# A state-space block that steps four tokens at a time, in a two-block transformer kernel

## The chip, the cores and the metric

The kernel runs on one core of one Trainium2 chip. The metric is the device time of the whole kernel in microseconds. A core has TensorE (PE in the profile), VectorE (DVE), ScalarE (ACT), GpSimd (POOL) and SyncE (SP); the last one here issues nearly all transfers between HBM and SBUF. Each engine runs its own instructions in the order in which the program lists them and waits on semaphores for the others.

## The reference

The program computes two blocks of a network for 256 tokens of width 1024. The first block is FFN, mixer, FFN and a gated embedding; the mixer projects the tokens and feeds a sparse attention (nsa, 8 heads) and a state-space path (s5), whose outputs are joined and projected by `w_out`. The second block has two layers with a context of 256 tokens; its context projections need nothing of the first block. The change concerns the state space:

```python
def s5_mixer(u, a_re, a_im, log_dt, b_re, b_im, c_re, c_im, d_skip, w_glu, b_glu):
    uf = u.reshape(B, L, S5_GROUPS, S5_GROUP)             # 32 groups of 16 channels
    a_bar = jnp.exp(lam * dt)                             # 64 complex states per group
    b_coef = (a_bar - 1.0) / lam
    bu = lax.complex(bu_re, bu_im) * b_coef
    _, state = lax.associative_scan(combine, (a_seq, bu), axis=1)   # x[t] = a x[t-1] + bu[t]
    y = real(state) @ c_re - imag(state) @ c_im + d_skip * uf
    y = jax.nn.gelu(y.reshape(B, L, S5_WIDTH))
    return y * jax.nn.sigmoid(y @ w_glu + b_glu)
```

## The kernel before

Activations lie transposed, channels on partitions and the 256 tokens along the free axis. A large product is made of three fp32r matmuls per weight tile (`mm3`, L360 to L363): high half times high half, high times low, low times high. `split` (L334) loads a weight tile `raw` through SP, ScalarE rounds it to `hi` (L349), and the low half `lo` = raw - hi is made by VectorE or, in every fourth tile of the mixer (`EV_MX` = 4, `self.every`), by GpSimd (L355).

`mixer_in` (L587) normalises h (`sumsq`, `rstd`; the sum over partitions is the matmul `bs`, its input is GpSimd's `acc`), projects u (`ev_u` writes `uT`, L619), then q, k and v (`mmb`, `mma` with `Ah`/`Al`), and then calls `s5` (L744), `nsa` (L844), `ctx_proj` of the second block, and after them `glu` (L796) and the output projection `mmo` (L652 to L655).

`s5` handles 16 pairs of groups, four in each of four steps j. Two matmuls `pbu` give the real and imaginary input of 128 states (two groups of 64) for 256 tokens. VectorE multiplies by the cosine and sine of the state's phase (`s5co`, `s5si`: a rotating frame in which the recurrence is real), GpSimd adds the pairs (L776, L777), two scans over 256 tokens run on VectorE (L780, L781), four products rotate back, GpSimd adds (L787, L788), and two matmuls `psy` multiply with the output matrix. A gelu writes the result over `uT`.

`nsa` first makes compressed keys and values (`compress`: 16 matmuls `cps` each, on weights `cw`), their softmax (`psc`, `pst`), and then for each i of four head pairs and each t of two token halves: scores `psS` (PE), mask and maximum (VectorE, L930), exponentials (ScalarE, L935), division and gate (VectorE, L937 to L941), transposes `psT` (PE), a copy `pT` (ScalarE), the product with the values `psO` (PE), and the halves `Ah`, `Al` of the result (L959, L960).

The order of the work on each engine is set at build time by a scheduler that goes through the program's instructions by priority (program order) and its own durations, within what buffers allow. A pool hands out its buffers in program order, and a tile waits until the tile that had the buffer is released. The PSUM pool `sm` has two buffers and serves `bs`, `psr`, `cps`, `psc`, `pst`, `psT` and `psO` alike; `mm` has two for `mmb`, `mma`, `mmo`; `s5p` holds `pbu` and `psy`. The matmuls of `ctx_proj` (`mmb` and `mma` with `Bh`/`Bl`, 384 and 96 of them) depend on nothing of the mixer and stand in PE's order wherever there is room. At the mixer's end `wmod` (L1020 and after) of the second block streams in, into memory that the attention used; `after` and `gate` (L1063 to L1068) tie such loads to an earlier instruction.

Of the kernel before, what the change touches and what calls it, by code (L numbers as in the profile page):

```python
# [137 lines left out]
def _layout(i):  # L138
# [48 lines left out]
    b = np.zeros((4, 4, 2, 16, 2, 2, 64), np.float32)  # L187
    c = np.zeros((2, 64, 16, 2, 2, 16), np.float32)
    for r, nm in enumerate(("re", "im")):
        bb = i[f"s5_b_{nm}"][0].reshape(4, 4, 2, 64, 16)  # L190
        cc = i[f"s5_c_{nm}"][0].reshape(16, 2, 16, 64)
        for gg in range(2):
            b[:, :, gg, :, r, gg, :] = bb[:, :, gg].transpose(0, 1, 3, 2)
            c[gg, :, :, r, gg, :] = cc[:, gg].transpose(2, 0, 1)
    a["s5b"] = b.transpose(1, 2, 3, 0, 4, 5, 6).reshape(128, 4, 2, 128)
    a["s5c"] = c.reshape(128, 16, 2, 32)
# [43 lines left out]
class Kern:  # L240
# [346 lines left out]
    def mixer_in(self, h, p):  # L587
# [54 lines left out]
        with (  # L642
            tc.tile_pool(name="s5", bufs=2) as sp,
            tc.tile_pool(name="nsa", bufs=2) as np_,
            tc.tile_pool(name="s5p", bufs=1, space=PSUM) as self.s5p,
        ):
# [1090 lines left out]
```

## Time and profile before

| | us |
|---|---|
| median of 3 runs (lowest to highest) | 1577.16 (1574.52 to 1580.79) |
| the profiled execution, its time | 1584.19 |
| the profiled execution, its span | 1582.0 |
| TensorE busy | 1513.8 |
| VectorE busy | 1183.3 |
| ScalarE busy | 873.7 |
| GpSimd busy | 356.9 |
| mean granted TensorE clock | 0.984 |

All rows that follow come from one profiled execution, and times in them count from the start of its span. Busy time of PE is modelled at its end and overlaps weight loads (PEld, the loading of the stationary operand); where PE works without a gap, weight loads are as dense as matmuls, so PEld shows how full PE is. The landmarks of the stretch that the change rewrites are: u is projected from about 206, the last matmul of the projections starts at 253.34, the first matmul of the GLU at 427.23, and the attention's last instruction at 443.36.

### The profile page before, as it was taken

What the parts mean: (1) busy time and instruction counts of PE and PEld (TensorE: products, weight loads), DVE (VectorE), ACT (ScalarE), POOL (GpSimd) and SP (SyncE); (2) the same over time, 40 slices, a digit from 0 to 9 for tenths busy, and PEclk for the clock granted to TensorE, in tenths of its full rate; (3) what the DMA queues carried; (4) which work ended last, traced back from release to release, by engine and by line L of the source; (5) the groups of instructions that cost most, each with busy time, mean ns of one, the idle gap of its engine ahead of it and who ended that gap; (6) DMA issues with size and microseconds to landing.
All of it is one profiled execution on the core that took longest, in us unless ns stands there. A gap on an engine that the chain in (4) does not pass through costs nothing.

```text
span 1582.0 us, 28967 instructions
## 1 busy us (share of the span) xinstructions
PE 1513.8 (96%) x11058; PEld 1401.6 (89%) x11058; DVE 1183.3 (75%) x2103; ACT 873.7 (55%) x1563; POOL 356.9 (23%) x378
## 2 busy tenths in 40 slices
PE   7999999999989999998999899999999989999997
PEld 7999997676677999998999888989999889989997
DVE  7998778898778865666997767677766575777665
ACT  7644556445464554564454567675555555755553
POOL 3320145554331201031021232310030522200100
PEclk9999999999999999999999999999999999999999
DMA  7988565321178636668888664445466444544564
GB/s 262 321 305 293 171 207 166 109 80 62 48 241 297 212 127 181 193 193 296 274 285 255 199 196 149 159 149 164 140 210 195 155 146 161 166 155 127 160 183 144
DMA packets 100523, 298.19 MB, mean 188 GB/s; under 512 B 14944, under 2 KB 23520, under 8 KB 99744
## 3 DMA queue, kind: packets, MB, share of 16 engines
q1 hardware_dynamic: 99056, 290.66, 57.3%
q0 software_dynamic: 1328, 5.68, 1.1%
q8 instruction: 87, 1.43, 0.3%
q14 instruction: 52, 0.43, 0.1%
HBM read 292.10 MB, written 4.20 MB: 187 GB/s over the span
## 4 chain that ended last, share of the span: by engine, by line
PE 70%; DVE 13%; issue 4%; ACT 4%; DMA 4%; POOL 3%; SPq 0%; DVEq 0%; ACTq 0%; POOLq 0%
PE mmm L363 6%; PE mmm L361 6%; PE mmm L362 6%; PE mmb L363 4%; PE mmb L362 4%; PE mmb L361 4%; DVE lo L355 4%; PE mmf L362 4%; PE mmf L363 4%; PE mmf L361 4%; PE mma L362 3%; PE mma L361 3%; PE mma L363 3%; PE mm L362 1%; PE mm L361 1%
## 5 line engine op out<-in xcount | busy, mean ns | idle before, releaser
L355 DVE TENSOR_TENSOR lo<-raw,hi 128x1024 fp32r<-128x1024 f32 (+3 forms) x483 | 549.9, 1141 | 226.8 <-ACT hi L349 225.2
L349 ACT CAST hi<-raw 128x1024 fp32r<-128x1024 f32 (+4 forms) x495 | 474.7, 963 | 403.6 <-PE mmm L362 80.9
L362 PE MATMUL mmb<-Bl,hi 128*128 128x256 f32 x576 | 167.8, 292 | 3.2 <-DVE Bl L409 3.2
L363 PE MATMUL mmb<-Bh,lo 128*128 128x256 f32 x576 | 167.9, 292 | 2.1 <-POOL lo L355 2.0
L361 PE MATMUL mmb<-Bh,hi 128*128 128x256 f32 x576 | 167.2, 292 | 2.7 <-DVE sdk L1302 2.4
L363 PE MATMUL mmm<-Bh,lo 128*128 128x256 f32 x576 | 163.6, 284 | 0.4 <-DVE lo L355 0.4
L361 PE MATMUL mmm<-Bh,hi 128*128 128x256 f32 x576 | 163.0, 283 | 0.3 <-DVE sgmg L1324 0.3
L362 PE MATMUL mmm<-Bl,hi 128*128 128x256 f32 x576 | 162.5, 282 | 0.0
L361 PEld LDWEIGHTS mmb<-Bh,hi 128*128 128x128 f32 x576 | 111.1, 194 | 8.1 <-issue 6.1
L363 PEld LDWEIGHTS mmb<-Bh,lo 128*128 128x128 f32 x576 | 111.6, 194 | 7.3 <-issue 3.9
L362 PEld LDWEIGHTS mmb<-Bl,hi 128*128 128x128 f32 x576 | 111.5, 194 | 7.3 <-DVE Bl L409 3.6
L361 PE MATMUL mmf<-Ah,hi 128*128 128x256 f32 x352 | 100.2, 285 | 10.0 <-ACT Ah L415 7.9
L363 PEld LDWEIGHTS mmm<-Bh,lo 128*128 128x128 f32 x576 | 108.5, 188 | 0.7 <-DVE lo L355 0.6
L361 PEld LDWEIGHTS mmm<-Bh,hi 128*128 128x128 f32 x576 | 108.6, 188 | 0.5 <-DVE sgmg L1324 0.5
L362 PEld LDWEIGHTS mmm<-Bl,hi 128*128 128x128 f32 x576 | 108.5, 188 | 0.0
L361 PE MATMUL mmf<-Bh,hi 128*128 128x256 f32 x352 | 100.8, 286 | 4.5 <-ACT hi L349 4.5
L1039 DVE CUSTOM_DVE_ANT_0 mw<-mw,cb 128x1024 f32<-128x1024 f32 x72 | 90.5, 1258 | 18.2 <-DMA mw<-wmod 13.1
L363 PE MATMUL mmf<-Bh,lo 128*128 128x256 f32 x352 | 100.7, 287 | 1.6 <-DVE lo L355 1.5
L361 PE MATMUL mm<-gh,hi 128*128 128x256 f32 x352 | 99.8, 284 | 1.8 <-DVE fo L545 1.8
L362 PE MATMUL mm<-gl,hi 128*128 128x256 f32 x352 | 99.6, 283 | 1.8 <-DVE gl L526 1.8
L362 PE MATMUL mmf<-Al,hi 128*128 128x256 f32 x352 | 100.4, 285 | 0.3 <-DVE Al L416 0.3
L363 PE MATMUL mmf<-Ah,lo 128*128 128x256 f32 x352 | 100.2, 285 | 0.3 <-DVE lo L355 0.3
(564 smaller groups left out, 4343.4 us busy)
## 6 DMA issues: line engine op xcount, KB each, us to landing
raw<-w SPq DMA_DIRECT2D x120, 512.0 KB, 5.0
raw<-wB SPq DMA_DIRECT2D x76, 512.0 KB, 3.8
mw<-wmod SPq DMA_DIRECT2D x72, 512.0 KB, 5.1
raw<-wml SPq DMA_DIRECT2D x72, 512.0 KB, 3.5
raw<-wbo SPq DMA_DIRECT2D x72, 256.0 KB, 2.7
raw<-wo SPq DMA_DIRECT2D x24, 512.0 KB, 4.3
raw<-w SPq DMA_DIRECT2D x16, 384.0 KB, 4.0
raw<-w_inB SPq DMA_DIRECT2D x12, 512.0 KB, 4.1
```

The source lines that it names most:

```text
L349: nc.scalar.copy(hi[:, :n], raw[:, :n])
L355: eng.tensor_tensor(lo[:, :n - cut], raw[:, :n - cut], hi[:, :n - cut].bitcast(F32), op=ALU.subtract)
L361: nc.tensor.matmul(ps, lh, rh, start=start, stop=False)
L362: nc.tensor.matmul(ps, lh, rl, start=False, stop=False)
L363: nc.tensor.matmul(ps, ll, rh, start=False, stop=stop)
L1039: nc.vector.tensor_tensor_reduce(o, w, cb[:, j - j0, :], 1.0, 0.0, ALU.mult, ALU.add, mod[:, m, j:j + 1])
```

## The change

Four tokens become one step. The tokens of a channel are regrouped so that the four of a step (s) lie on different partitions and the 64 steps (k) along the free axis: `ev_u` writes `uT` in the order (s, k), and the new `s5_load` sends it to HBM (`s5d`) and back into `u4`, 32 channels by four tokens on the 128 partitions, with one write and four reads for each half of the channels, on SP. From powers of a up to the fourth, `s5_setup` builds `z`; for each j, `s5` builds from `x` and `z` the input tables `bx` and the output tables `cx` (VectorE: `s5m`, then sums and differences on 64 partitions), transposes `bx` (`s5pt`, copied by ScalarE to `s5br4`), and multiplies `bx` with `cx` for what tokens of one step give to each other (`s5pk`, copied into `tw`). Both `s5pt` and `s5pk` take their PSUM from `sm`. Then 8 matmuls `pbu` of 64 columns, the rotation, two scans over 4 x 64 columns (with `rt` zero at each first column), the rotation back, and 12 matmuls `psy`. All pair sums are on VectorE. The result goes back to `uT` through HBM, one write and four reads for each two j, on GpSimd's queue, still in the order (s, k); `glu` puts the tokens in order while it reads. `EV_MX` is 0, so GpSimd makes no low half in the mixer. The pool of `s5` is opened ahead of the projections, and `compress` takes its weight buffers from the tag `pT` instead of `cw`.

```diff
@@ flags @@
-EV_CB, EV_B2, EV_F2, EV_MX = 0, 0, 0, 4
+EV_CB, EV_B2, EV_F2, EV_MX = 0, 0, 0, 0
@@ mixer_in @@
+        s5 = contextlib.ExitStack()
+        sp = s5.enter_context(tc.tile_pool(name="s5", bufs=1))
+        self.s5p = s5.enter_context(tc.tile_pool(name="s5p", bufs=1, space=PSUM))
...
         def ev_u(i, ps):
-            nc.vector.tensor_tensor(uT[:, 2 * i:2 * i + 2, :], ps, rb2, op=ALU.mult)
+            nc.vector.tensor_tensor(uT[:, 2 * i:2 * i + 2, :].rearrange("p a (s k) -> p a k s", s=4),
+                                    ps.rearrange("p a (k s) -> p a k s", s=4),
+                                    rstd.rearrange("p (k s) -> p k s", s=4)[:, None].to_broadcast([128, 2, 64, 4]),
+                                    op=ALU.mult)
+            self.s5_load(sp, uT, i)
@@ s5_load, new @@
+        js = slice(2 * jj, 2 * jj + 2)
+        d = self.s5d[jj]
+        self.nc.sync.dma_start(d, uT[:, js, :])
+        for k in range(4):
+            self.nc.sync.dma_start(self.u4[32 * k:32 * k + 32, js],
+                                   d[:, :, 64 * k:64 * k + 64].rearrange("(q c) j k -> c j q k", q=4))
@@ s5, tables of one j @@
+            for ri in range(2):
+                m = [sp.tile([128, 5, 8, 16], F32, tag=f"s5m{n}", name="s5m", bufs=1) for n in range(2)]
+                for n in range(2):
+                    tt(m[n], x[:, n, pr].rearrange("p a b c -> p (a b) c")[:, None].to_broadcast([128, 5, 8, 16]),
+                       z[:, n ^ ri, :, pr, :].rearrange("p s a b -> p s (a b)")[:, :, :, None].to_broadcast([128, 5, 8, 16]),
+                       ALU.mult)
+                for g in range(2):
...
+                    tt(bx[ri][gs, :, :, gc], v[0][gs, 0, :, 0:4, :], v[1][gs, 0, :, 0:4, :], op)
+                    tt(cx[ri][gs, :, :, gc], v[0][gs, 1], v[1][gs, 1], op)
+            for ri in range(2):
+                pt = self.sm.tile([128, 512], F32, tag="sm", name="s5pt")
+                for q in range(4):
+                    nc.tensor.transpose(pt[:, 128 * q:128 * q + 128], bx[ri][:, q].rearrange("p s c -> p (s c)"), ident)
+                nc.scalar.copy(br[:, ri], pt.rearrange("p (a b) -> p a b", a=4))
+            pt = self.sm.tile([128, 512], F32, tag="sm", name="s5pk").rearrange("p (a b) -> p a b", a=4)
...
+            for k in range(4):
+                ks = slice(32 * k, 32 * k + 32)
+                nc.scalar.copy(tw[ks, :, 32 * k:], pt[0:32, :, 0:128 - 32 * k])
@@ s5, pair sums (G is GpSimd, V and tt VectorE) @@
-                G.tensor_tensor(t1, t1, t2, op=ALU.add)
-                G.tensor_tensor(t3, t3, t4, op=ALU.subtract)
...
+            tt(t1, t1, t2, ALU.add)
+            tt(t3, t3, t4, ALU.subtract)
@@ s5, the way back @@
+            if j % 2:
+                js = slice(j - 1, j + 1)
+                d = self.s5d[2 + j // 2]
+                nc.gpsimd.dma_start(d, u4[:, js].rearrange("p j q k -> p j (q k)"))
+                for q in range(4):
+                    nc.gpsimd.dma_start(uT[32 * q:32 * q + 32, js, :].rearrange("c j (s k) -> c j s k", s=4),
+                                        d[:, :, 64 * q:64 * q + 64].rearrange("(s c) j k -> c j s k", s=4))
@@ compress @@
-            raw = p.tile([128, 4, T], F32, tag="cw", name="cw", bufs=2)
+            raw = p.tile([128, 4, T], F32, tag="pT", name="cw")
```

How instructions move, at three places. On PE, in the middle of the stretch of the state space, the first attention half-blocks of the kernel before stand between the context matmuls (`mmb` with `Bh`) and the state space (`pbu`, `psy`):

```order
L363 MATMUL mmb_4761<-Bh_2356,lo_4794 128x256
L361 MATMUL mmb_4761<-Bh_2356,hi_4793 128x256
L953 MATMUL psO_4059<-pT_4082,vtok_2749 128x2x128 x2
L955 MATMUL psO_4059<-pcT_4057,vcm_4017 128x2x128
L948 MATMUL psT_4115<-cst0_97,s__4092 128x128
L770 MATMUL pbu_3688<-uT_2746,braw_2474 128x256 x2
L948 MATMUL psT_4115<-cst0_97,s__4092 128x128 x2
L789 MATMUL psy_3603<-s5u1_3632,cr_2477 32x256
L948 MATMUL psT_4115<-cst0_97,s__4092 128x128
L928 MATMUL psS_4140<-kk_2748,qT_2747 128x128
L928 MATMUL psS_4145<-kk_2748,qT_2747 128x128
L790 MATMUL psy_3603<-s5u3_3634,ci_2478 32x256
```

In the changed kernel, PE at the last tables of the state space and the first `cps` of the compressed keys:

```order
L804 MATMUL s5pk_3682<-s5cx1_3335,s5bx1_3333 32x128
L357 MATMUL mmb_4760<-Bh_2360,hi_4792 128x256
L358 MATMUL mmb_4760<-Bl_2361,hi_4792 128x256
L359 MATMUL mmb_4760<-Bh_2360,lo_4793 128x256
L357 MATMUL mmb_4760<-Bh_2360,hi_4792 128x256
L358 MATMUL mmb_4760<-Bl_2361,hi_4792 128x256
L359 MATMUL mmb_4760<-Bh_2360,lo_4793 128x256
L357 MATMUL mmb_4760<-Bh_2360,hi_4792 128x256
L358 MATMUL mmb_4760<-Bl_2361,hi_4792 128x256
L359 MATMUL mmb_4760<-Bh_2360,lo_4793 128x256
L822 MATMUL pbu_3706<-s5u4_2899,s5br4_3669 128x64 x7
L905 MATMUL cps_3776<-cw_3777,blk_3767 30x256 x4
```

and PE after the GLU's last matmul, where the attention now stands:

```order
L953 MATMUL psc_3878<-kcm_3816,qT_2763 128x15 x8
L953 MATMUL psc_3887<-kcm_3816,qT_2763 128x15 x8
L977 MATMUL pst_3911<-cst0_97,pcm_3898 128x128 x4
L1015 MATMUL psT_3942<-cst0_97,s__3919 128x128 x4
L995 MATMUL psS_3999<-kk_2764,qT_2763 128x128
L995 MATMUL psS_4004<-kk_2764,qT_2763 128x128
L1020 MATMUL psO_3918<-pT_3941,vtok_2765 128x2x128 x2
L1022 MATMUL psO_3918<-pcT_3916,vcm_3876 128x2x128
L1015 MATMUL psT_3974<-cst0_97,s__3951 128x128 x4
L995 MATMUL psS_4031<-kk_2764,qT_2763 128x256
L995 MATMUL psS_4036<-kk_2764,qT_2763 128x256
L1015 MATMUL psT_3980<-cst0_97,s__3951 128x128 x4
```

What moved: in the kernel before `cps` of k begins with the end of the projections and the attention is spread over the rows of the context matmuls; now `cps` of k follows the last `s5pk`, and the eight half-blocks, but for some first scores, follow the GLU with 18 `mmo` matmuls between them.

On VectorE, around the evacuation of u (`uT`), before:

```order
L355 TENSOR_TENSOR lo_2972<-raw_2970,hi_2971 128x1024
L466 RECIPROCAL rstd_2794<-sd_2795 128x256
L355 TENSOR_TENSOR lo_3012<-raw_3010,hi_3011 128x1024
L612 TENSOR_TENSOR cosr_2811<-cst3_2744,rstd_2794 128x256
L613 TENSOR_TENSOR sinr_2812<-cst3_2744,rstd_2794 128x256
L619 TENSOR_TENSOR uT_2746<-mmb_2815,rstd_2794 128x512
L619 TENSOR_TENSOR uT_2746<-mmb_2877,rstd_2794 128x512
L355 TENSOR_TENSOR lo_3082<-raw_3080,hi_3081 128x1024
```

and now, with the tables of j = 0 and the first product of j = 1 (`s5m`) ahead of it:

```order
L770 TENSOR_TENSOR s5bx1_3333<-s5m_3350,s5m_3351 64x16x16
L438 TENSOR_SCALAR rc_2819<-psr_2816 128x2
L770 TENSOR_TENSOR s5cx1_3335<-s5m_3350,s5m_3351 64x20x16
L818 SCALAR_TENSOR_TENSOR s5ph_3386<-cst0_97,s5r_2423 128x256
L351 TENSOR_TENSOR lo_2938<-raw_2936,hi_2937 128x1024
L816 TENSOR_SCALAR s5co_3384<-s5co_3384 128x256
L611 TENSOR_TENSOR cosr_2833<-cst3_2760,rstd_2810 128x256
L612 TENSOR_TENSOR sinr_2834<-cst3_2760,rstd_2810 128x256
L770 TENSOR_TENSOR s5m_3444<-s5x_2476,s5z_2499 128x640
L770 TENSOR_TENSOR s5m_3445<-s5x_2476,s5z_2499 128x640
L602 TENSOR_SCALAR rch_2822<-rc_2819 128x2
L617 TENSOR_TENSOR uT_2762<-mmb_2837,rstd_2810 128x2x64x4
```

What moved: the low half and the evacuation stand behind products and sums of the tables (`s5m`, `s5bx`, `s5cx`), which the kernel before did not have; most of the tables of j = 0 stand in the 20 rows above these.

On GpSimd, before, at the end of the state space (`L312` loads constants of the second block):

```order
L788 TENSOR_TENSOR s5u3_3852<-s5u3_3852,s5u4_3853 128x256
L776 TENSOR_TENSOR s5t1_3862<-s5t1_3862,s5t2_3863 128x256
L777 TENSOR_TENSOR s5t3_3864<-s5t3_3864,s5t4_3865 128x256
L787 TENSOR_TENSOR s5u1_3879<-s5u1_3879,s5u2_3880 128x256
L788 TENSOR_TENSOR s5u3_3881<-s5u3_3881,s5u4_3882 128x256
L355 TENSOR_TENSOR lo_5141<-raw_5139,hi_5140 128x1024
L312 DMA cst1_5444<-cst1 128x516
L1068 COPY cb_6510<-go_320 128x1
```

and now, the whole way back between two memsets and the same load:

```order
L930 MEMSET hidv_3819 128x512
L958 MEMSET pcm_3898 128x512
L854 DMA s5d2_112<-s5u4_2899 128x512
L856 DMA uT_2762<-s5d2_112 32x8x64 x4
L854 DMA s5d3_113<-s5u4_2899 128x512
L856 DMA uT_2762<-s5d3_113 32x8x64 x4
L308 DMA cst1_5303<-cst1 128x516
L1135 COPY cb_6369<-go_324 128x1
```

What moved: the sums are gone from GpSimd, and ten transfers stand ahead of the load of constants.

## Rows read from the trace of the kernel before

**Rows 1.** The page: busy time and instructions by engine; the chain that ended last.

```profile
PE 1513.8 (96%) x11058; PEld 1401.6 (89%) x11058; DVE 1183.3 (75%) x2103; ACT 873.7 (55%) x1563; POOL 356.9 (23%) x378
...
PE 70%; DVE 13%; issue 4%; ACT 4%; DMA 4%; POOL 3%; SPq 0%; DVEq 0%; ACTq 0%; POOLq 0%
```

**Rows 2.** Busy us, instructions by stretch, then granted clock, DMA share, GB/s.

```profile
60.00:180.00 120.00, 118.19 (x988) 118.02 (x987) 103.19 (x185) 56.63 (x82) 16.20 (x18) 0.99 0.81 279
225.00:253.50 28.50, 28.50 (x213) 25.36 (x211) 19.96 (x34) 17.65 (x27) 9.29 (x7) 1.00 0.51 157
253.50:427.20 173.70, 168.53 (x857) 115.58 (x856) 153.45 (x352) 88.81 (x176) 88.06 (x78) 0.95 0.29 91
...
475.00:520.00 45.00, 41.47 (x203) 34.03 (x203) 39.22 (x69) 21.52 (x41) 8.32 (x5) 1.00 0.85 291
```

**Rows 3.** Single PE instructions (start, us); PE's waits; one stretch at half clock.

```profile
253.57 2.34 PE L838 MATMUL cps<-cw,blk 128*30 128x256 f32 x10
...
426.88 0.60 PE L948 MATMUL psT<-cst,s__4291 128*128 128x128 f32 x4
...
PE pbu L770 <- DVE s5t L746: 1.7, 1, 1.7
...
355.00:360.00 5.00, 5.00 (x21) 3.63 (x21) 5.00 (x16) 0.59 (x1) 2.64 (x4) 0.50 0.32 105
```

**Rows 4.** VectorE's groups, 253 to 428: count, busy us, mean ns, idle before.

```profile
L355 DVE TENSOR_TENSOR lo<-raw,hi 128x1024 fp32r<-128x1024 f32 x18 | 24.3, 1352 | 1.8 <-ACT hi L349 1.8
L780 DVE TENSOR_TENSOR_SCAN s5zr<-s5r,s5t 128x256 f32<-128x256 f32 x16 | 14.1, 879 | 0.0
...
L746 DVE TENSOR_TENSOR s5u<-s5zi,s5co 128x256 f32<-128x256 f32 x16 | 11.9, 746 | 0.0
...
L746 DVE TENSOR_TENSOR s5u<-s5zr,s5si 128x256 f32<-128x256 f32 x16 | 6.6, 410 | 0.0
```

**Rows 5.** GpSimd's groups, 200 to 470.

```profile
L355 POOL TENSOR_TENSOR lo<-raw,hi 128x1024 fp32r<-128x1024 f32 x11 | 28.5, 2593 | 34.7 <-ACT hi L349 34.7
...
L787 POOL TENSOR_TENSOR s5u<-s5u,s5u 128x256 f32<-128x256 f32 x16 | 16.5, 1029 | 43.6 <-DVE s5u L746 43.6
```

**Rows 6.** Single instructions of GpSimd and VectorE, 256 to 266.

```profile
256.12 2.38 POOL L355 TENSOR_TENSOR lo<-raw,hi 128x1024 fp32r<-128x1024 f32 x1 [3.63 <-ACT hi L349]
...
256.61 2.18 DVE L765 TENSOR_SCALAR s5co<-s5co 128x512 f32<-128x512 f32 x1 [0.31 <-ACT s5co L764]
...
265.43 0.41 DVE L765 TENSOR_SCALAR s5co<-s5co 128x512 f32<-128x512 f32 x1
```

**Rows 7.** GpSimd's DMA issues (ns min/median/max); its transfers, us to landing.

```profile
L312 POOL DMA_DIRECT2D cst<-cst x2: 600/604/609, 208.3 to 442.7; - x2
...
pT<-pT POOLq DMA_DIRECT2D x1, 256.0 KB, 4.8
```

**Rows 8.** Groups of the attention on VectorE, then on ScalarE.

```profile
L960 DVE TENSOR_TENSOR Al<-psO,Ah 64x256 fp32r<-64x256 f32 x5 | 2.1, 417 | 0.4 <-ACT Ah L959 0.4
...
L930 DVE CUSTOM_DVE_ANT_0 s__4246<-psS,cst 128x256 f32<-128x256 f32 x4 | 1.6, 398 | 0.0
...
L941 DVE TENSOR_TENSOR s__4246<-s__4246,l 128x1024 f32<-128x1024 f32 x1 | 1.2, 1211 | 0.0
...
L949 ACT COPY pT<-psT 128x512 f32<-128x512 f32 x12 | 7.0, 582 | 16.3 <-PE psT L948 16.2
...
L935 ACT ACTIVATE s__4246<-s__4246,mx 128x256 f32<-128x256 f32 x4 | 2.0, 496 | 1.7 <-DVE mx L932 1.7
...
L935 ACT ACTIVATION_READ_ACCUMULATOR s__4246<-s__4246,mx 128x1 f32 x4 | 0.7, 187 | 0.0
```

**Rows 9.** The u evacuation on VectorE: start, us of both.

```profile
222.69 1.28 DVE L619 TENSOR_TENSOR uT<-mmb,rstd 128x512 f32<-128x512 f32 x2
```

**Rows 10.** The attention's last instruction, and the first load of wmod.

```profile
443.36 0.43 DVE L960 TENSOR_TENSOR Al<-psO,Ah 64x256 fp32r<-64x256 f32 x1
...
443.91 0.43 SPq L1035 DMA_DIRECT2D mw<-wmod  x1
```

More of the change, by code (lines that the diff above doesn't have):

```diff
@@ L158, in _layout @@
     put("bglu", _cols(i["s5_b_glu"][0]))
-    put("s5d", _cols(i["s5_d"][0].reshape(-1)))
+    put("s5d", np.tile(i["s5_d"][0].reshape(16, 32).T, (4, 1)))
     put("are", _cols(i["s5_a_re"][0].reshape(-1)))
@@ L186, in _layout @@
     a["wcv2"] = i["cmp_wv2"][0].reshape(2, 128, 64).transpose(1, 0, 2)
-    b = np.zeros((4, 4, 2, 16, 2, 2, 64), np.float32)
-    c = np.zeros((2, 64, 16, 2, 2, 16), np.float32)
+    x = np.zeros((2, 64, 2, 16, 2, 16), np.float32)
     for r, nm in enumerate(("re", "im")):
[L190 to L196, printed above, removed]
+        x[:, :, r, :, 0] = i[f"s5_b_{nm}"][0].reshape(16, 2, 64, 16).transpose(1, 2, 0, 3)
+        x[:, :, r, :, 1] = i[f"s5_c_{nm}"][0].reshape(16, 2, 16, 64).transpose(1, 3, 0, 2)
+    a["s5x"] = x.reshape(128, 2, 16, 2, 16)
     a["wglu"] = _wb(i["s5_w_glu"][0])
@@ L281, in run @@
             self.spill = [dram.tile([128, 8, T], F32, name=f"spill{n}") for n in range(2)]
+            self.s5d = [dram.tile([128, 2, T], F32, name=f"s5d{n}") for n in range(4)]
             self.grow = dram.tile([8, 128], F32, name="grow")
@@ L641, in mixer_in @@
         opair = self.new_pair(8, "A")
[L642 to L646, printed above, removed]
+        with s5, tc.tile_pool(name="nsa", bufs=2) as np_:
             self.s5(sp, uT)
@@ new lines, in s5_setup, with cmul @@
+        nc.scalar.copy(P[:, 1, 1], s1)
+        tmp = [tp.tile([128, 5, 16], F32, tag=f"s5tm{n}", name="s5tm", bufs=1) for n in range(2)]
+        def cmul(o, x_, y_, n, neg=False):
+            m, w = tmp[0][:, :n], tmp[1][:, :n]
+            tt(m, x_[0], y_[0], ALU.mult)
+            tt(w, x_[1], y_[1], ALU.mult)
+            tt(o[0], m, w, ALU.subtract)
+            tt(m, x_[0], y_[1], ALU.mult)
+            tt(w, x_[1], y_[0], ALU.mult)
+            if neg:
+                V.scalar_tensor_tensor(o[1], m, -1.0, w, op0=ALU.mult, op1=ALU.subtract)
+            else:
+                tt(o[1], m, w, ALU.add)
@@ new lines, in s5 @@
+        f, r, x, z = self.s5t
+        u4 = self.u4
+        ident = self.c("ident")
+        t1_ = self.c("t1")[:, None, 0:64].to_broadcast([128, 4, 64])
+        W = lambda nm: sp.tile([128, 4, 64], F32, tag="s5w", name="s5" + nm, bufs=5)
+        bx = [sp.tile([128, 4, 4, 32], F32, name=f"s5bx{n}", bufs=1) for n in range(2)]
+        cx = [sp.tile([128, 4, 5, 32], F32, name=f"s5cx{n}", bufs=1) for n in range(2)]
+        tw = sp.tile([128, 4, 128], F32, name="s5tw", bufs=1)
+        for t in (*bx, *cx, tw):
+            nc.gpsimd.memset(t, 0.0)
```

157 lines of the change are left out of this document (84 added, 73 removed).

## The prediction

> **What bounds the kernel now.** I read the page first, then busy time by stretch, then the groups of the stretch that the change rewrites, and last the single instructions on both sides of it. The page says TensorE: 1513.8 us of 1582, and 70% of the chain that ended last [rows 1]. That is an average. In a stage of plain matmuls PE loads weights without a break, 118.02 us in 120 for 987 of them, so 0.12 us for one 128x256 matmul [rows 2]. In the stretch 253.5 to 427.2, which holds the state-space block, most of the attention and the second block's first projections, weight loads fill only 115.58 of 173.7 us while VectorE is busy for 153.45 [rows 2]. There VectorE sets the pace, and PE's "busy" is stretched by waiting.
>
> How much of it is PE's own work? The stretch's order has 384 matmuls mmb (128x256) and 96 mma (128x512, priced double): 46 + 23 = 69 us. A float32 matmul of 256 columns leaves two records; ten records of cps took 2.34 us, so 0.47 each, and four transposes took 0.60, of which about 0.13 each is pace [rows 3]. With 30 pbu, 32 psy, 25 cps, 16 wide and 14 narrow psS, 24 psO, 44 transposes and 16 tiny psc that is another 74: **143 us of PE work in 173.7**, 31 lost. VectorE's share comes from the state space: 16 passes of two scans at 0.88, and products at 0.41 when undisturbed but 0.75 when not [rows 4]. Summed over its groups it is about 108 us. GpSimd adds 11 low halves of 2593 ns and pair sums for which it waits 43.6 us on VectorE [rows 5].
>
> **The change, part by part.**
>
> *State space on VectorE.* Per j there are now 23 operations of 128x256 at a pace of 0.34 (an estimate from 0.41 less the overlap that the rows' starts show), two scans at 0.6, four products of 128x640 (estimated 0.85 each from 1.35 for 128x1024 [rows 4]) and eight sums on 64 partitions at about 0.45: 7.8 + 1.2 + 3.4 + 3.6 = 16, so 64 for four j against 108. Saved: 44 us, nearly all inside the VectorE-paced stretch. The 12 low halves that come over from GpSimd cost 12 x 1.25 = 15 us there.
>
> *Stalls between GpSimd and VectorE.* One VectorE operation, 128x512 on one input, took 2.18 us while GpSimd's low half ran, and 0.41 nine us later [rows 6]. These stalls go with GpSimd's work; up to 1.8 us for each of 11 low halves is some 15 us, which about pays for the 15 above. So VectorE's load in the stretch falls from 153 to about 80 us (the attention's part leaves it too, see below), and PE becomes the bound there.
>
> *Order on PE: the attention leaves the stretch.* This decides. The tables s5pt and s5pk take the PSUM ring sm (two buffers, handed out in program order), and so do cps, psc, psT and psO of the attention, which the program asks for later. So cps of k comes only behind the last s5pk, as the changed order shows, and the eight attention half-blocks, which stood among 480 second-block matmuls, now stand after the GLU, in PE's rows almost bare: 18 mmo matmuls between them. All second-block matmuls are used up before.
>
> The stretch from the projections' end to the GLU then holds 69 us of those matmuls, 95 small float32 matmuls (pbu, psy, pk) at 0.23, half of a cps (bounds 0.13, a transpose, and 0.47, a cps: 12 to 45 us), 24 transposes, 24 cps and a few psS: 69 + 22 + 3 + 11 + 2 = **107 us**. What is lost on top was 31 of 143 before, 22%. With VectorE at 80 of 107 I take 10%, so **118** (bounds: 107, nothing lost, and 131, the same share).
>
> *GLU.* The way back: GpSimd issues one write and four reads per half. An issue took 0.60 us [rows 7], a transfer of 256 KB on its queue 4.8 us to land [rows 7]. 0.6 + 4.8 + 4 x 0.6 + 4.8 = 12.6 after the last gelu, which itself follows the last psy by some 4. PE has about 11 us of work to put in front of the GLU (cps, the tail of mmb). Wait: 12.6 + 4 - 11 = 5 (0 if the small reads land in 2 us and the write too, 12 if they queue one behind the other). Behind the waiting mmb on PE stands everything: attention and mmo. The GLU itself with eight cps in it is 48 x 0.12 + 8 x 0.47 = 9.5, say 10.
>
> The Trainium skill, SBUF — State Buffer, section "SBUF: two separate sides", says of a DMA issued from GpSimd's queue that its descriptors are written by GpSimd's cores, which some VectorE operations lock out, and names 620 against 3100 ns. By that page five DMAs might take 12 us more, an estimate, and the sum below would end at +20; the trace's two issues of 600 and 609 ns [rows 7] ran beside a busy VectorE and do not show it. The mechanism is the slower rival's, below.
>
> *Bare attention.* PE's rows from the GLU to the last psO hold 14 wide and 12 narrow psS, 32 psO, 52 transposes, psc and 18 mmo: 39 us at the prices above. But they hang on each other: a wide half-block is four score reductions (0.4 each), four exponentials with their sums (0.50 + 0.19), the three operations on l, 1.21 for the product, transposes, pT 0.58, psO, Ah, and Al 0.42 [rows 8]. In series this is 1.9 + 2.8 + 0.5 + 1.2 + 2.4 (two rounds of transposes and copies) + 2.4 + 0.8 = 12 us; a narrow one 8. VectorE alone has 8.0 us per pair, ScalarE 7.6, PE 9.8. Two buffers let the next half-block start under the former, so I take 10.9 per pair, a little over PE's 9.8, and 11 for the head (psv, psc, its softmax on VectorE, pst, pcT, in series): 11 + 4 x 10.9 = **55** (46, if PE's work sets it with the head half hidden, to 62, where half of each narrow chain is exposed).
>
> *Projections.* The tables of j = 0 are put ahead of the u evacuation on VectorE (uT, at 222.69 before [rows 9]): 8 us of products and sums in front of it. s5pt stands on PE in the middle of the projections, and PE waits there for the tables; bs stands 27 rows earlier, before acc is likely done. VectorE is busy for only 19.96 of 28.5 [rows 2], which absorbs a part. I take **+6** (0 to 10). The s5d writes and reads on SP stall only weight loads that lie two tiles ahead: nothing.
>
> *After the attention.* Its end, Al at 443.36, also frees the memory for wmod, whose first load is issued at 443.91 [rows 10]; from there to 520 VectorE is busy for 39.22 of 45 [rows 2], with the same work in both kernels. So what the attention's end moves, the end moves. Low halves from GpSimd there: +1.
>
> *Clock.* After gaps of PE the granted clock falls to the lower level: one row here shows 0.50 from 355 to 360 [rows 3], after a wait of 1.7 us for a product of VectorE. The new gaps (s5pt, GLU, bare attention) are at least as many: **+3** (0 to 10).
>
> Sum: 253.4 + 6 + 118 + 5 + 10 + 55 = 447.4 against 443.4, +4; +3 and +1 make **+8 us** of the profiled execution, 1584.19 with a span of 1582.0. The median of the runs shown is 1577.16, so 1577.16 + 8 = **1585**.
>
> **The rivals.**
>
> *A, the forecast:* the 44 us that VectorE saves come out of the stretch, and the attention gives them back, bare: 1585, own range 1576 to 1594.
>
> *B, faster:* PE's work sets the time throughout. Projections +3, 108 for the stretch (nothing lost but 1%), no wait at the GLU to speak of (2), 10, and 49 for the attention: 253.4 + 3 + 108 + 2 + 10 + 49 = 425.4, 18 earlier; +3 for clock and halves: -15, **1562**. For it: VectorE's load falls by half, and no engine is then over 75% in the stretch. Against it: only 18 matmuls fill the attention.
>
> *C, slower:* the return path and the bare attention both pay. The five GpSimd DMAs follow one another with their landings, wait 12 instead of 5, and after that gap the attention's matmuls run at the lower clock: 39 us of work, of which a third at twice the price is 13 more. +8 + 7 + 13 = +28; half of the second hidden behind VectorE's chain, **+21, 1598**. It decides from the point where PE stands still for more than a us or two between half-blocks. For it: 0.50 in [rows 3]. Against it: fill-in from mmo.
>
> *D, nothing moves:* the stretch's saving and the attention's loss cancel, or the regrouped block costs VectorE what it saved (operands with strides, 64-partition sums at twice my price: 8 x 0.45 x 4 = 14, gone, and 131 for the stretch with 49 behind it): **1577**, within 4.
>
> **How the numbers follow.** A 0.50, B 0.24, C 0.16, D 0.10. About 0.5% (7.9 us) is what a measurement of this kernel can tell from no change. Of A about half lies beyond +7.9, so slower is 0.26 + 0.16 = 0.42, same 0.24 + 0.10 = 0.34, faster 0.24. The range for 8 in 10 goes from B's 1562 to a little past C: 1562 to 1602.
>
> **What would show each step.** Right: between the projections' end and the first ygh matmul VectorE at some 80 us busy and PE's weight loads above 85%; the first matmul of the GLU near 393 with a wait for a DMA or ygh; the last Al near 446 to 450, and from the GLU to there PE's weight loads below 75%, waiting for l, pT and s_. Wrong: if the last Al comes before 435, the attention's chains overlap better than I hold; if the stretch still takes over 135 us, the tables on VectorE, the ScalarE copies or the chain of one j are the new pace; if PE waits for no table at s5pt, the +6 falls.

## The result and the profile after

The changed kernel takes **1601.01 us** (median of 4 runs, 1600.52 to 1602.93), the kernel before 1576.41 (median of 4 runs). The ratio is 1.0142, 95% interval 1.0122 to 1.0161: slower by 24.6 us, where 8 had been forecast. The side is right, and the time lies at the edge of the range of 1562 to 1602, but the size is wrong by a factor of three.

The two traces show 17 us of the 24.6, spans of 1599.0 against 1582.0. The other 7 or so stand in no row: the execution of the kernel before that was profiled took 1584.19, 7.8 above the median of its runs, and one trace can't say which of its stretches was the long one.

Where the time went is told by six landmarks (start of the instruction, us):

| | before | forecast | after |
|---|---|---|---|
| last matmul of the projections | 253.3 | 259.4 | 256.3 |
| first matmul of the GLU | 427.2 | 382.4 | 370.3 |
| last matmul of the GLU | 435.4 | 392.4 | 380.3 |
| last Al of the attention | 443.4 | 447.4 | 461.9 |
| last addition to h behind mmo | 474.8 | | 494.9 |
| span | 1582.0 | | 1599.0 |

So the state space saved more than I had said: the GLU comes 57 us earlier than before. The attention, which then stands alone, gives back all of that and 18 us more. Everything behind it moves along.

The page of the changed kernel shows it at a glance: busy time by engine, the granted clock of TensorE in 40 slices of 40 us, in tenths, and the chain that ended last.

```profile
PE 1520.7 (95%) x11186; PEld 1424.5 (89%) x11186; DVE 1153.9 (72%) x2078; ACT 872.7 (55%) x1575; POOL 252.5 (16%) x295
...
PEclk9999999997678999999999999999999999999999
...
PE 76%; DVE 10%; ACT 4%; DMA 4%; issue 3%; POOL 1%; SPq 0%; DVEq 0%; ACTq 0%; POOLq 0%
```

GpSimd lost 104 us of work against [rows 1], VectorE 29, and PE won nothing by it. The slices from 360 to 480, where the kernel before shows 9 throughout, show 7, 6 and 7 (and the next one 8): PE ran at the lower of its two clocks for a good part of them.

The next view is busy time by stretch (PE, weight loads PEld, VectorE, ScalarE, GpSimd; then granted clock, DMA share, GB/s). The stretches end at the projections' end, at the last context matmul, at the first matmul of the GLU, at its last, and then at the last Al of each of the four pairs of half-blocks.

```profile
225.00:256.30 31.30, 31.12 (x258) 30.78 (x257) 19.65 (x28) 21.00 (x33) 5.62 (x6) 1.00 0.72 218
256.30:361.40 105.10, 102.37 (x733) 90.89 (x731) 84.61 (x172) 54.53 (x83) 3.64 (x6) 1.00 0.47 151
361.40:370.30 8.90, 7.82 (x33) 3.89 (x31) 4.58 (x15) 5.42 (x18) 2.41 (x4) 0.81 0.47 143
370.30:380.40 10.10, 9.82 (x65) 7.33 (x64) 2.53 (x9) 2.47 (x5) 0.00 (x0) 1.00 0.44 145
380.40:414.80 34.40, 25.52 (x106) 18.73 (x104) 17.51 (x56) 13.16 (x39) 0.00 (x0) 0.65 0.14 46
414.80:431.90 17.10, 15.10 (x50) 9.05 (x50) 6.56 (x29) 6.23 (x21) 0.00 (x0) 0.64 0.00 0
431.90:451.50 19.60, 18.30 (x49) 10.46 (x48) 6.37 (x27) 6.22 (x21) 0.00 (x0) 0.50 0.00 0
451.50:462.30 10.80, 8.21 (x35) 5.42 (x33) 3.51 (x12) 4.39 (x14) 1.01 (x4) 0.89 0.09 13
```

Compare the second row with the third of [rows 2]. Weight loads now fill 90.89 of 105.1 us, 86%, and VectorE is busy for 84.61; the stretch runs at PE's pace, as forecast. (Up to the first matmul of the GLU, the stretch that the forecast had named, it is 94.78 of 114.0, 83%, and 89.19.) Then read the last four rows downwards. The third pair ran wholly at half clock and took 19.6 us: twice the 9.8 us of PE work that the prediction counted for a pair, and PE is busy for 18.30 of them. The fourth, most of it at the full clock, took 10.8, where 10.9 was forecast. PE "busy" alone would mislead: the 93% of the third pair are short work stretched by the clock, as its groups show (name, shapes, count, then busy us and mean ns):

```profile
L1020 PEld LDWEIGHTS psO<-pT,vtok 128*128 128x128 f32 x10 | 3.1, 332 | 1.2 <-issue 0.6
...
L1020 PE MATMUL psO<-pT,vtok 128*128 128x256 f32 x11 | 5.5, 649 | 0.0
```

In the third pair of run e9 (below), all of it at the full clock, the same two groups of psO read:

```profile
L1023 PEld LDWEIGHTS psO<-pT,vtok 128*128 128x128 f32 x12 | 2.1, 190 | 0.5 <-issue 0.3
...
L1023 PE MATMUL psO<-pT,vtok 128*128 128x256 f32 x12 | 3.3, 388 | 0.0
```

A weight load takes 332 ns at half clock and 190 at the full one, a matmul record 649 and 388. That is two thirds and more on top of each record, and no engine but PE is near its limit: VectorE works for 6.37 of 19.6 us, ScalarE for 6.22.

The four results themselves, on VectorE (start, duration; the second half of each pair):

```profile
414.38 0.43 DVE L1027 TENSOR_TENSOR Al<-psO,Ah 64x256 fp32r<-64x256 f32 x1
...
431.49 0.43 DVE L1027 TENSOR_TENSOR Al<-psO,Ah 64x256 fp32r<-64x256 f32 x1
...
451.08 0.43 DVE L1027 TENSOR_TENSOR Al<-psO,Ah 64x256 fp32r<-64x256 f32 x1
...
461.91 0.43 DVE L1027 TENSOR_TENSOR Al<-psO,Ah 64x256 fp32r<-64x256 f32 x1 [0.31 <-ACT Ah L1026]
```

PE's waits from 380 to 415 (us in total, times, longest) show what the head of the bare attention adds to that: compressed values whose gelu comes out only behind the GLU, and their softmax.

```profile
PE pst L977 <- DVE pcm L973: 3.9, 1, 3.9
PE psv L941 <- ACT hidv L934: 2.0, 2, 1.5
PE psS L995 <- DVE mx L997: 1.8, 2, 1.4
PE cpt L910 <- DVE mx L999: 1.1, 1, 1.1
```

### The profile page after: what moved, and what is told of

The parts are those of the page before. It is cut to its first block, busy times and chain, and to the rows that moved or that the text cites. A ratio compares the mean times of both kernels' runs of the same rounds, so it can differ in the third digit from the quotient of the medians.

```text
span 1599.0 us, 29155 instructions
## 1 busy us (share of the span) xinstructions
PE 1520.7 (95%) x11186; PEld 1424.5 (89%) x11186; DVE 1153.9 (72%) x2078; ACT 872.7 (55%) x1575; POOL 252.5 (16%) x295
## 4 chain that ended last, share of the span: by engine, by line
PE 76%; DVE 10%; ACT 4%; DMA 4%; issue 3%; POOL 1%; SPq 0%; DVEq 0%; ACTq 0%; POOLq 0%
PE mmm L359 6%; PE mmm L358 6%; PE mmm L357 6%; PE mmf L359 5%; PE mmf L358 5%; PE mmf L357 4%; PE mmb L359 4%; PE mmb L358 4%; PE mmb L357 4%; PE mma L358 3%; PE mma L357 3%; PE mma L359 3%; DVE lo L351 3%; PE mm L357 2%; PE mm L358 2%
## 5 line engine op out<-in xcount | busy, mean ns | idle before, releaser
L351 DVE TENSOR_TENSOR lo<-raw,hi 128x1024 fp32r<-128x1024 f32 (+4 forms) x495 | 560.5, 1135 | 232.9 <-ACT hi L345 231.2
L359 PE MATMUL mmb<-Bh,lo 128*128 128x256 f32 x576 | 164.1, 286 | 2.5 <-DVE lo L351 2.4
L358 PE MATMUL mmf<-Bl,hi 128*128 128x256 f32 x352 | 99.8, 284 | 0.0
```

The lines of the kernel that those rows point to most:

```text
L351: eng.tensor_tensor(lo[:, :n - cut], raw[:, :n - cut], hi[:, :n - cut].bitcast(F32), op=ALU.subtract)
L358: nc.tensor.matmul(ps, lh, rl, start=False, stop=False)
L359: nc.tensor.matmul(ps, ll, rh, start=False, stop=stop)
```

## The experiments

Two theories stood at the start. ORDER: the tables took the attention's company away through the PSUM ring sm, and alone on PE it runs at half clock. BLOCK: the regrouped state space and its transfers cost what was lost. ORDER has two parts, the place and the clock, and each has its own runs. All ratios are to the kernel before on the same chip.

### e1: the tables take other PSUM buffers

```diff
-                pt = self.sm.tile([128, 512], F32, tag="sm", name="s5pt")
+                pt = self.s5p.tile([128, 512], F32, tag=("psy", "pbu")[ri], name="s5pt")
...
-            pt = self.sm.tile([128, 512], F32, tag="sm", name="s5pk")
+            pt = self.s5p.tile([128, 512], F32, tag="psy", name="s5pk")
```

> The changed kernel with one thing undone: s5pt and s5pk take the PSUM buffers of psy and pbu instead of the ring sm, so that cps, psc, psT and psO of the attention no longer queue behind the tables. By its order cps of k stands at the end of the projections again and the half-blocks stand among the context matmuls. Theory ORDER (the attention lost its company on PE, and alone it runs at the lower granted clock): PE's work from 256 on is 107 + 10 + 39 = 156 us; with a tenth lost the last Al comes at 256 + 170 = 426, 36 us earlier than in the changed kernel, and the time is 1601 - 36 = 1565, in 1555 to 1575, under the kernel before. Granted clock above 0.98. Theory BLOCK (the regrouped state space and its transfers cost what was lost): 1595 to 1603, unchanged.

Measured: 1568.81 us, ratio 0.9947 (0.9925 to 0.9969), the last Al at 427.3 where 426 was expected. The place of two tiles turns 24 us of loss into 8 of gain. Busy time by stretch, from the projections' end to the GLU, the GLU, and 24 us behind it:

```profile
255.30:417.30 162.00, 158.48 (x967) 128.32 (x967) 110.34 (x288) 82.42 (x181) 6.04 (x10) 0.95 0.34 109
417.30:426.00 8.70, 8.70 (x66) 7.88 (x65) 3.40 (x5) 5.16 (x10) 0.42 (x3) 1.00 0.65 202
426.00:450.00 24.00, 18.56 (x129) 17.65 (x128) 21.63 (x49) 18.26 (x47) 5.17 (x6) 0.86 0.80 285
```

State space, attention and context matmuls together take 162 us at a granted clock of 0.95; apart, in the changed kernel, they took 105.1 + 8.9 + 81.9. BLOCK falls: with tables and transfers unchanged the kernel is faster than before. The clock of the whole program is 0.983, so "above 0.98" just holds.

### e2: the ring alone, in the kernel before

```diff
-                pb = self.s5p.tile([128, 512], F32, name="pbu").rearrange("p (a b) -> p a b", a=2)
+                pb = self.sm.tile([128, 512], F32, tag="sm", name="pbu").rearrange("p (a b) -> p a b", a=2)
```

> The kernel before with one thing added: its pbu takes PSUM from the ring sm. Nothing else of the state space is changed, but the ring now puts the attention behind the last pbu and, by the order, behind the GLU, with 18 mmo matmuls in it as in the changed kernel. Theory ORDER: the state-space stretch loses the attention's 32 us of VectorE, so the GLU starts near 395 to 400; the bare attention takes 82 as in the changed kernel: last Al near 487 to 492 instead of 443, time 1577 + 45 = 1622, in 1605 to 1635; the granted clock shows 0.5 in the attention. Theory BLOCK: the place of the attention is worth little, 1570 to 1585.

Measured: 1638.96 us, ratio 1.0383 (1.0354 to 1.0413), 60 us slower, a little outside the expected 1605 to 1635. Nothing of the state space's arithmetic was touched. Stretches to the GLU, the GLU, and then to the last Al of each of the four pairs:

```profile
253.50:400.30 146.80, 123.17 (x634) 86.12 (x634) 128.33 (x239) 56.62 (x80) 85.06 (x78) 0.88 0.31 103
400.30:408.00 7.70, 7.67 (x56) 6.73 (x56) 4.89 (x15) 5.92 (x18) 1.10 (x1) 1.00 0.23 84
...
408.00:455.60 47.60, 35.50 (x139) 23.21 (x138) 18.73 (x61) 13.35 (x42) 1.28 (x1) 0.71 0.16 57
455.60:469.50 13.90, 11.80 (x51) 7.22 (x50) 6.59 (x29) 6.22 (x21) 0.00 (x0) 0.88 0.00 0
469.50:483.10 13.60, 11.60 (x50) 7.34 (x50) 6.40 (x27) 6.21 (x21) 0.00 (x0) 0.87 0.00 0
483.10:495.50 12.40, 8.23 (x33) 5.69 (x31) 3.53 (x11) 4.40 (x14) 1.02 (x4) 0.86 0.07 19
```

The GLU starts at 400.3 as expected, and the bare attention takes 87.5 us. So the place is a cause by itself: putting the attention behind the GLU costs the kernel before even more than the changed one, whose faster state space pays for part of it.

But the 87.5 us are not made like the 81.9 of the changed kernel. All `cps` of the compressed values stand behind the GLU here, and PE waits 4.9 us for their weights, so that the head and the first pair take 47.6. The other three pairs, bare as they are, run near the full clock (0.86 to 0.88) and take 13.9, 13.6 and 12.4. The clock of 0.5 that was expected in the attention shows in its head alone (0.50 from 430 to 450).

```profile
PE cps L838 <- DMA cw<-wcv: 4.9, 1, 4.9
```

### e3: more work on PE in the bare attention

```diff
+        spare = self.s5p.tile([128, 512], F32, tag="psy", name="spare")
+        for _ in range(6):
+            nc.tensor.matmul(spare[:, 0:256], vcm, qT[:, 0, :], start=True, stop=True)
...
                    nc.scalar.copy(pT[:, kt, :, :, :], pt)
+                    nc.tensor.matmul(spare, vtok[:, kt, 0:128], pT[:, kt].rearrange("p r e q -> p (r e q)"), start=True, stop=True)
```

> The changed kernel with more work on PE: in the bare attention one float32 matmul of 512 columns for each pT copy (12 in all) and six of 256 columns ahead of the first half-block, written to a PSUM buffer that nobody reads. About 14 us of work at the full clock. Theory CLOCK (the 82 us of the attention are long because PE runs at the lower clock there): busier PE keeps the clock, the attention takes 60 to 72 instead of 82 though it has more to do, time 1580 to 1592. Theory CHAIN (the hand-offs between engines set the 82 us, the clock is only a sign of an idle PE): the added work stands in the chain between pT and psO, time 1601 to 1613.

Measured: 1594.97 us, ratio 1.0115 (1.0080 to 1.0151), against 1.0142 of the changed kernel. This is between the two expectations and decides little: the spare matmuls stand between pT and psO, so what the clock gives back they take.

### e5 and e9: the same work where it stands in nobody's chain

```diff
                nc.tensor.matmul(po[:, :, ts_], vcm[a:a + 32, :], pcT[a:a + 32, :, ts_], start=False, stop=True,
                                 tile_position=(a, 0))
+                for _ in range((2, 3)[t]):
+                    nc.tensor.matmul(spare, vtok[:, 0, 0:128], pT[:, 0].rearrange("p r e q -> p (r e q)"), start=True, stop=True)
```

In the head there are twelve spare matmuls; e9 has `(1, 1)[t]` in place of `(2, 3)[t]`.

> The changed kernel with more work on PE again, but behind psO of each half-block, where it stands in nobody's chain: two float32 matmuls of 512 columns behind each narrow half-block, three behind each wide one, and twelve of 256 columns in the head, written to a PSUM buffer that nobody reads; some 25 us of work at the full clock on top of 39. Theory CLOCK (of the 82 us from the GLU's last matmul to the last Al, the part over 55 comes from the lower clock): the granted clock stays near 1 from the head on, PE's 64 us with the first waits set the time, 68 to 76 us and not 82; time 1587 to 1595. Theory CHAIN: the clock is no cause, and the added work fills gaps or lengthens: 82 to 105 us, time 1601 to 1624.

> The kernel of e5 with less added work: one spare matmul of 512 columns behind each half-block (1.9 us for each pair of half-blocks instead of 4.7), the twelve in the head as there. In the changed kernel the four results Al lie 16.3 us apart at the lower clock; in e5 14.8 us at the full clock with 4.7 us of added work. Theory CLOCK: where the clock stays full, a pair is 14.8 - 4.7 + 1.9 = 12.0 us, and the last Al comes 8 us earlier than in e5, time near 1588; where 1.9 us is too little to keep the clock, pairs of 16 to 18 us stand beside rows at 0.5, 1596 to 1604. Theory CHAIN: pairs of 14 to 16 us whatever the clock shows.

Measured: e5 1597.88 us, ratio 1.0118 (1.0096 to 1.0140); e9 **1590.17 us**, ratio 1.0074 (1.0050 to 1.0098). The four pairs of e5, by busy time and clock (from the GLU's end to the last Al of each):

```profile
382.30:420.70 38.40, 33.62 (x142) 24.45 (x140) 17.71 (x56) 13.25 (x40) 0.00 (x0) 0.78 0.12 41
420.70:438.10 17.40, 16.28 (x73) 9.44 (x72) 9.04 (x40) 9.31 (x36) 0.00 (x0) 1.00 0.01 1
438.10:450.30 12.20, 11.94 (x49) 7.06 (x48) 3.70 (x15) 2.78 (x7) 0.00 (x0) 1.00 0.00 1
450.30:463.50 13.20, 10.81 (x43) 6.33 (x41) 3.49 (x11) 4.37 (x14) 1.00 (x4) 1.00 0.05 17
```

and of e9:

```profile
382.30:418.10 35.80, 30.95 (x136) 23.22 (x134) 17.65 (x56) 13.21 (x40) 0.00 (x0) 0.76 0.14 44
418.10:434.30 16.20, 13.75 (x55) 7.67 (x54) 6.45 (x29) 6.21 (x21) 0.00 (x0) 0.89 0.00 1
434.30:448.60 14.30, 11.95 (x54) 7.23 (x54) 6.22 (x26) 6.21 (x21) 0.00 (x0) 1.00 0.00 1
448.60:460.20 11.60, 8.29 (x37) 5.19 (x35) 3.54 (x11) 4.43 (x14) 1.00 (x4) 1.00 0.09 16
```

In e5 the three later pairs take 42.8 us with 4.7 us of added work each, in e9 42.1 with 1.9, in the changed kernel 47.5 with none: with more to do and at a higher clock, less time. The third pair shows it best. PE has the same instructions in the same order in e9 and in the changed kernel, but for the spare ones (VectorE's order differs in a few small operations). It takes 14.3 us at 1.00 instead of 19.6 at 0.50, though PE waits longer in it, 2.2 us instead of 1.3. So the clock is a cause in the pairs, and CHAIN, which gave it no share, falls in that form.

The size is another matter. For e9 CLOCK had said 12.0 us for a pair and a last Al 8 us ahead of e5's; CHAIN had said pairs of 14 to 16. The pairs took 16.2 (at 0.89), 14.3 and 11.6, on average 14.0, and the last Al came 3.4 us ahead (459.75 against 463.11). At the full clock a pair is thus longer than the forecast's 10.9, as in e2, and the hand-offs between the engines have their share. Net of the added work the three pairs would be 28.7 us in e5 and 36.4 in e9; but some of that work may have filled waiting time, so these are lower bounds and no prices.

e5's own expectation (68 to 76 us from the GLU to the last Al, 1587 to 1595) failed: it took 81. The head ran at half clock up to 403 in spite of the added work, and its twelve spare matmuls took 7.9 us there and held up `pst`, which starts at 405.1 instead of 399.2.

The whole times of e3, e5 and e9 say less of the clock than the pairs do. The spare matmuls changed the order of the work behind the attention too: from the last Al on VectorE has one order in these three runs and another in the changed kernel, and from 495 on so has PE. From the last Al to the end of the span it is 1137.0 us in the changed kernel and 1134.6, 1130.4 and 1132.1 in e3, e5 and e9. Of the 7.1 us between e9's span (1591.9) and the changed kernel's only 2.2 lie ahead of the last Al, and 4.9 behind it, which neither theory had said. So it was in part luck that e9 met the time expected where the clock stays (near 1588).

### e4 and e7: the low halves

```diff
-EV_CB, EV_B2, EV_F2, EV_MX = 0, 0, 0, 4
+EV_CB, EV_B2, EV_F2, EV_MX = 0, 0, 0, 0
```

e4 is this edit alone in the kernel before; e7 is e1 with the edit undone.

> The kernel before with EV_MX = 0 alone: the 12 low halves of GpSimd in the mixer go to VectorE. Theory ORDER says nothing of it but that it isn't the cause: VectorE gets 15 us in a stretch where it sets the pace and loses the stalls beside GpSimd's low halves (up to 1.8 us each of 11): -5 to +8, so 1572 to 1585. If the halves were a cause of the loss it would be 1590 or more.

> The kernel of e1 (tables in the PSUM of psy and pbu) with EV_MX = 4: every fourth low half of the mixer on GpSimd again. VectorE is no longer the pace there (about 92 of 171 us busy), so relieving it by 15 us gives nothing, and a GpSimd half takes 2.5 us where VectorE's takes 1.2 and slows VectorE beside it: 1566 to 1576, no gain on 1569.

Measured: e4 1577.90 us, ratio 0.9998 (0.9983 to 1.0012); e7 1569.25 us, ratio 0.9951 (0.9930 to 0.9972), against 0.9947 of e1. The low halves are worth nothing in either kernel. In e4's trace VectorE makes 27 of them instead of 20 from the projections' end to the last Al, 34.6 us against 26.8, and is busy for less in all, 161.2 against 165.7: what it takes over it saves elsewhere. That these are the stalls beside GpSimd's low halves is a reading; no run separates them. In e7 VectorE isn't the bound (busy for 109.8 of 161 us from 256 to 417).

### e6: the way back on SyncE's queue

```diff
-                nc.gpsimd.dma_start(d, u4[:, js].rearrange("p j q k -> p j (q k)"))
+                nc.sync.dma_start(d, u4[:, js].rearrange("p j q k -> p j (q k)"))
```

and likewise for the four reads.

> The changed kernel with the way back (one write and four reads for each two j) issued on SyncE's queue instead of GpSimd's. In the trace of the changed kernel the last way back takes from 360.8 to about 368.6, and PE fills it with cps at the lower clock. Rival QUEUE (GpSimd's queue is slow and holds up the GLU): the way back shrinks by 2 to 4 us and the kernel gains as much, 1596 to 1599. Theory ORDER: GpSimd's queue is not the cause of the loss; 1597 to 1606, since SyncE also holds weight loads behind its waits.

Measured: 1602.57 us, ratio 1.0139 (1.0113 to 1.0166): no gain. Issues and the end of the last way back in the changed kernel (GpSimd's queue; ScalarE's ygh is the first reader):

```profile
360.80 0.58 POOL L854 DMA_DIRECT2D s5d<-s5u  x1 [36.26 <-DVE s5u L850]
364.39 2.41 POOL L856 DMA_DIRECT2D uT<-s5d  x4 [3.01 <-DMA s5d<-s5u]
...
368.55 1.19 ACT L866 CAST ygh<-uT 128x256 fp32r<-128x256 f32 x2 [2.15 <-DMA uT<-s5d]
```

and in e6:

```profile
361.83 0.33 SPq L854 DMA_DIRECT2D s5d<-s5u  x1
...
365.87 2.54 SPq L856 DMA_DIRECT2D uT<-s5d  x4
...
370.45 1.17 ACT L866 CAST ygh<-uT 128x256 fp32r<-128x256 f32 x2
```

On GpSimd's queue the way takes 7.8 us from the first issue to the reader, on SyncE's 8.6. The queue is not a cause.

### e8: the first tables later

```diff
-        for t in (*bx, *cx, tw):
+        for t in (bx[1], *cx, tw):
             nc.gpsimd.memset(t, 0.0)
+        for n in range(2):
+            nc.gpsimd.tensor_tensor(bx[0][:, 2 * n:2 * n + 2].rearrange("p a b c -> p (a b c)"), self.rs_, self.rs_, op=ALU.subtract)
```

The base is e1; `rs_` is rstd.

> The kernel of e1 with the first tables held back: half of s5bx is cleared by GpSimd as rstd - rstd instead of a memset, so that the tables of j = 0 can't be finished before rstd, and by the order the evacuation of u now stands ahead of s5bx. This tests the term for the projections, where PE's wait for bs, s5pt and a low half cost about 3.3 us between 205 and 225. Expected: -2 to -4 us, 1564 to 1568; if u's evacuation was never late for PE, 1569 to 1572.

Measured: **1558.10 us**, ratio 0.9861 (0.9845 to 0.9877), the fastest of all. But not for the reason that was tested. The last matmul of the projections starts at 254.6 against 255.0 in e1, so the term that I meant to test is worth 0.4 us. The gain of 11 comes from another place in the order, which the edit moved by accident: the GLU now stands ahead of the last half-blocks.

```profile
254.90:404.70 149.80, 148.95 (x951) 122.77 (x951) 109.47 (x282) 78.74 (x168) 6.04 (x10) 0.95 0.35 113
404.70:416.00 11.30, 11.30 (x77) 9.27 (x76) 7.84 (x19) 8.70 (x20) 0.00 (x0) 1.00 0.50 179
416.00:450.00 34.00, 29.36 (x208) 26.96 (x207) 26.15 (x54) 24.11 (x59) 9.62 (x12) 0.95 0.66 231
```

In e1 the GLU ends the chain, and PE waits for its results, with nothing beside them to do (e1, 420 to 445):

```profile
PE mmo L358 <- DVE Al L879: 3.1, 1, 3.1
PE mmo L357 <- ACT gt L875: 2.3, 1, 2.3
```

In e8 the wait for Al of the GLU is gone and the one for gt is 0.3, since attention and mmo stand behind the GLU. At the last Al of the attention e8 is 1.7 us ahead of e1 (425.6 against 427.3), at the last addition to h 9.1 (453.6 against 462.7). That the 11 us are all of this is read from the traces, and no run separates it.

## Why the prediction was wrong, step by step

**What bounds the kernel now: right.** VectorE set the pace of the stretch [rows 2], and 31 us were lost there on top of PE's 143.

**State space on VectorE: right.** The groups of the changed kernel (count, busy us, mean ns) have the prices taken: 0.82 for a 128x640 product (0.85 taken), 0.49 for the longer sums on 64 partitions (0.45), 0.68 for a scan (0.6).

```profile
L351 DVE TENSOR_TENSOR lo<-raw,hi 128x1024 fp32r<-128x1024 f32 x24 | 29.3, 1221 | 2.7 <-ACT hi L345 2.6
L770 DVE TENSOR_TENSOR s5m<-s5x,s5z 128x640 f32<-128x640 f32 x10 | 7.8, 820 | 0.0
L770 DVE TENSOR_TENSOR s5cx<-s5m 64x320 f32<-64x320 f32 x12 | 5.8, 485 | 0.6 <-PE psy L844 0.5
...
L831 DVE TENSOR_TENSOR_SCAN s5t<-s5ph,s5t 128x256 f32<-128x256 f32 x4 | 2.7, 685 | 0.0
```

VectorE is busy for 89.2 us up to the first matmul of the GLU where some 80 were forecast. The low half's mean is 1221 ns against 1352 in [rows 4], which fits the stalls beside GpSimd that were to go; e4 shows that the exchange was worth nothing in the kernel before.

**Stretch of the state space and wait at the GLU: too long by 9.** Forecast were 118 + 5 to the first matmul of the GLU, measured are 114.0. Most of the lost tenth was not lost. (The text also gave 393 as the time of the GLU's first matmul; by its own sum that is the GLU's end.) The way back left time before the GLU, but it was filled: PE had half of the cps of v to do, at the lower clock for a part (0.81 from 361.4 to 370.3), and waited 1.1 us in all.

**The way back.** It took 7.8 us where 12.6 were taken. The Trainium skill, SBUF — State Buffer, section "SBUF: two separate sides", names 3100 ns for a DMA of GpSimd's queue beside a VectorE operation that locks GpSimd out, against 620 alone. No run here shows such a price for the queue: from the issue of the write to that of the first read it is 3.6 us on GpSimd's queue and 4.0 on SyncE's (the rows of e6). The measurement decides: that rival is out in this kernel.

**Projections: right as a stage, by other waits.** Their last matmul starts 2.9 us later than before, but the changed kernel comes to them 3.2 us earlier (the same matmul of u's projection starts at 207.7 instead of 210.9), so the stage itself is 6.1 us longer where +6 was forecast. The 3.2 us were in no term. e2 and e4, with the old order up to there, don't have them: they are 0.8 us behind and 0.1 ahead of the kernel before. PE's wait for tables at s5pt, which most of the term stood for and without which it was to fall, is not in the trace. PE waits for Ah instead, and for acc at bs, which the term had named; then it runs at half clock for most of ten us. In the kernel before PE waits for nothing between 206 and 253.

```profile
PE bs L446 <- POOL acc L429: 1.8, 1, 1.8
PE mmb L357 <- ACT Ah L411: 1.7, 1, 1.7
...
210.00:220.00 10.00, 8.16 (x43) 7.78 (x43) 9.85 (x18) 4.69 (x8) 3.02 (x4) 0.66 0.07 19
```

**Order on PE: right as a mechanism.** cps behind the last s5pk, the attention behind the GLU: e1 undoes it and e2 makes it alone (with the late `cps` of the values on top).

**Bare attention: the step that failed.** It was put at 55 us, 46 to 62, and took 81.9: +27, more than the whole error of the sum, which earlier terms cut to 14.5 at the last Al. By pairs: the head and the first pair took 34.4 instead of 21.9, the second 17.1, the third 19.6 and the fourth 10.8, each against 10.9.

The second and third give 15 of the 27. They ran at 0.64 and 0.50, where PE's 9.8 us of work cost up to twice that and PE became the bound; the prices of [rows 3] could not show it, since they were read at the full clock. (By those prices PE's work behind the GLU adds up to some 37 us, not 39; that is not what failed.) In e2 the same two pairs took 13.9 and 13.6 at 0.88 and 0.87. So some 9 of the 15 us are the clock, and some 6 were missing from the price of a pair near the full clock as well, an estimate from e2.

The head gives 12. Its rows are both at half clock (0.65 over the stretch) and full of waits (8.8 us, above). PE is busy for 17.5 us between 385 and 408.5, at 0.51; half of that, 9 us, is the most that the full clock could have saved, an estimate. Of the waits the prediction had counted the softmax in its 11 us, but not the gelu of the compressed values, which comes out only behind the GLU (2.0 us at `psv`). How much of the 12 is clock and how much wait no run separates; that stays open.

**Clock: the right sign, the wrong kind of term.** I had priced it as +3 for the time after a gap, from one wait of 1.7 us and the stretch behind it [rows 3]. The projections show such a place. But in the bare attention the clock stays low for long while PE has work nearly all the time:

```profile
420.00:450.00 30.00, 28.02 (x76) 16.33 (x74) 9.22 (x38) 8.23 (x25) 0.00 (x0) 0.50 0.00 0
```

The price of such a stretch is PE's whole work a second time, and not some us behind each gap. Why the clock stays low here and not in the same pairs of e2, no run shows. Rival C had a part of this mechanism, at 13 us for a third of the work and half of that hidden, with 1598; it came closest and should have had the first place, though its other half, the slow way back, did not come. The Trainium skill, TensorE: Matmul & The Clock Gate, section "A second HAM failure mode: psum-queue depth-cycling", tells of a kernel whose PE, idle for moments between groups of matmuls, goes back and forth between the two clocks; the rows of the four pairs, 0.65, 0.64, 0.50 and 0.89, agree.

**The baseline.** Seven of the 24.6 us were in the profiled execution of the kernel before, as told above. The forecast of +8 was made against that execution and put on the median; no term could see it.

## What to carry to other kernels

Before pricing a stage that a change leaves alone on TensorE, price it at the lower clock too; a stage with filler beside it and the same stage bare are two different stages. When a rewrite adds small PSUM tiles, look at which ring they are taken from and who stands behind them in program order: one ring of two buffers decided here between 24 us of loss and 8 of gain, with the same arithmetic. And when an experiment gains, look where: e8's 11 us were real and had nothing to do with the reason for which it was run, and more than half of what separates e9's trace from the changed kernel's lies behind the stage that e9 was to test, under another order of the work.

## What the runs showed of the hardware

Added work on TensorE can shorten a stage: with 1.9 us of spare matmuls in it a pair of half-blocks took 14.3 us at 1.00 (e9), bare 19.6 at 0.50. The same work in the head did not help: the twelve spare matmuls there took 7.9 us, and the clock stood at 0.50 from 390 to 400. A granted clock of 0.50 can stand for 30 us (420 to 450) beside a PE that the records show busy for nine tenths; what tells the state is the length of one record (psO: 649 ns at 0.50, 388 in a pair of e9 that ran at 1.00), not the busy share. A round trip of 256 KB through HBM with a regrouping of 32-partition blocks took 7.8 us on GpSimd's queue and 8.6 on SyncE's, and four reads issued back to back took 2.41 and 2.54 us of issue.
